# An attention stream in a hand-written order: projection matmuls moved out of the closing steps, the norm in seven pieces, subtractions moved from VectorE to GpSimd

## The chip, the cores and the metric

The kernel runs on one core of a Trainium2 chip. The metric is the device time of one execution in microseconds (us). The engines are TensorE (PE; its weight loads are listed apart as PEld), VectorE (DVE), ScalarE (ACT), GpSimd (POOL) and SyncE (SP), which here issues most DMAs. Each engine runs its own instructions strictly in the order in which the program lists them, and semaphores make one engine wait for another.

## The reference

One layer of a hybrid encoder over 16 learned "meta" tokens and 4096 tokens of width 1024. Cut to what matters:

```python
u = rmsnorm(h, norm_g)                       # h = meta tokens + x
f_in, f_gate, q, k, v, a_gate = split(u @ w_in)
f_out = fourier_branch(f_in) * silu(f_gate)  # real part of a 2-D DFT per group of 64 channels, then a mix
a_out = attention(q, k, v) * silu(a_gate)    # 8 query heads, 2 key/value heads of 64, bidirectional
h = h + concat(f_out, a_out) @ w_out
return rmsnorm(h, final_g)[:, 16:]
```

Queries and keys are normalised per head and rotated before the scores; the softmax runs over all 4112 positions. Inputs and result are float32, and the kernel reaches that precision with pairs of 16-bit numbers: a value is kept as a high part and the rest.

## The kernel before

**Phase A** (0 to about 715 us of the span) does the first norm and the input projection and writes queries, keys, values and gates to DRAM. The change does not touch it.

**The stream.** Phase B handles 8 blocks of 512 queries, and in each block four pairs of query heads: 32 pairs, `pairs = [(b, p)]`, numbered i. A pair is 66 steps j, 33 for each of its two heads, and n = j % 33. Step n = 0 takes the 16 meta keys; the other 32 steps take one tile of 128 keys each, in eight quads of four. In a quad the steps with n % 4 = 1 and 2 ("first" and "second") each open a score bank, a 128x512 float32 piece of PSUM from the pool `pq`, tag "s", which has two, with two 512-column matmuls: one with the high part of the queries (L1120) and one with their rest (L1121). Third and fourth steps (n % 4 = 3 and 0) add the difference to the key tile two steps before onto the same two banks (L1117). The fourth step is the closing one, and its numbers j are listed in `RUNS`. It also makes, in this order, two half-height matmuls for the rest of the differences (L1125), four half-height matmuls that estimate score maxima for a later pair into banks "m" of the pool `pm`, which has four (L1039), and the exponentials of both its last steps. Two relu/reduce pairs on these estimates (ACT `rl`, L1044; DVE `mx`, L1045) follow, one in the closing step, one in the next step.

Each step's exponential is an ACT instruction of 128x512 (`pe`, L1130). The part that the 16-bit `pe` loses is a subtraction `rr` of 128x512 (L1132) on DVE or POOL, as the set `on_dve` says. Five steps later (`LAG`) nine small matmuls multiply `pe` and `rr` by the values into bank `o` (L1147 to L1154). When a head ends, ACT copies `o` to `tt` (L1161), DVE makes a reciprocal and POOL four instructions on `ob`.

**Work laid between the steps.** The output projection of the previous block is 48 matmuls of 512 columns a pair (`po`, L1227) in two halves of 24, each half into one bank; DVE then takes the half out with the residual (`hh`, L1232). `OUT` lists the steps at which one projection matmul stands, right behind the step's score matmuls (`OUT0` does for pair 4, the first that has any). The final norm of the rows finished in the pair before is cut into pieces (`out_end`): a square on ACT, a guess, three Newton steps, and on DVE the scaling `yo` of 128x1024 (L1258) with the DMA out. They stand at the steps `NORM`. `out_tr` copies a pair's gated heads on ACT at step `TR` and sends them a step later through a transposing DMA (`at`, L1213) for the projection. Near the end of a pair `fin` turns the next pair's maxima into a row with one small matmul into an "m" bank (L1079), and `put` writes this row into the next queries with one copy on ACT and one on DVE (L1085, L1086).

**The Fourier branch** is a list of small entries, `flist`, filled by `f_fill` and drawn by `f_step(how many, ...)`: DFT matmuls `pd` (L858), gathers, transposes (`trans`) and mixes (`mix`: 24 matmuls, `mo` on ACT and POOL, and DMAs `mf_d` that are held until the next gather). Part of it is drawn while the first pair's maxima are made (the "startup", between phase A and the stream, `INIT` = 11 entries at a time), the rest at two or three entries a step in pairs 0 to 3 (`block0`).

The order of everything is written by hand: loop order in the code is the order on each engine. Nothing reorders it.

Of the kernel before, what the change touches and what calls it, by code (L numbers as in the profile page):

```python
# [22 lines left out]
F32 = mybir.dt.float32  # L23
# [4 lines left out]
ALU = mybir.AluOpType  # L28
# [4 lines left out]
P = 128  # L33
D = 1024
# [4 lines left out]
NT = 32  # L39
HD = 64  # L40
# [9 lines left out]
QB = 512  # L50
# [698 lines left out]
def phase_b(tc, a, pool, mm3, id32, id16, sc):  # L749
# [5 lines left out]
    V, S, T, G = nc.vector, nc.scalar, nc.tensor, nc.gpsimd  # L755
    dma, dma_t = nc.sync.dma_start, nc.sync.dma_start_transpose
# [3 lines left out]
    with ExitStack() as st:  # L760
        bp = pool(st, "bp")
        w1 = pool(st, "b1", 1)
# [3 lines left out]
        pm = pool(st, "pm", 4, PSUM)  # L766
        pq = pool(st, "pq", 2, PSUM)
# [38 lines left out]
        gts = {}  # L806
# [78 lines left out]
        def catch_up():  # L885
            while behind:
                behind.pop(0)()
# [76 lines left out]
        def f_fill():  # L964
            done = []
            for i, u in enumerate(seq):
                flist.append(("begin", i))
                flist.extend([("d", None)] * (50 if i > 8 else 52 if u is LAST else 26))
                flist.append(("gather", i))
                if i != 8:  # L970
                    done.append((len(flist), i))
                flist.extend([("gap", None)] * (12 if i == 8 else int(8 < i < 17)))

            for pos_, i in reversed(done):
                end = len(flist)
                flist.insert(min(pos_ + (21 if i < 8 else 34), end), ("t", (mix, i)))
                flist.insert(min(pos_ + (8 if i < 8 else 13), end), ("t", (trans, i)))

        f_fill()
# [115 lines left out]
        def stream(i):  # L1095
            b, p = pairs[i]
            kv = p // 2
            if p == 0:
                obs[b] = w2.tile([P, 4, 512], F32, tag="ob", name="ob")
            ob = obs[b]  # L1100
            out = []
            for e in range(2):
                h = 2 * p + e
                qa, qb = qA[b % 2][:, h], qB[b % 2][:, h]
                acc, banks = [], {}
                for t, n in enumerate(SEQ):
                    out.append(step(h, kv, t, n, qa, qb, acc, banks, ob, gts[i][:, :, e * HD:(e + 1) * HD]))
            return out

        def step(h, kv, t, n, qa, qb, acc, banks, ob, gate):  # L1110
            d = {}
            cs = slice(n * P, (n + 1) * P)

            def qk():
                if n < NT and n % 8 >= 4:
                    s = d["s"] = banks.pop(n - 4)
                    T.matmul(s, K[kv][:, 0, cs], qa, start=False, stop=False, skip_group_check=True)  # L1117
                else:
                    s = d["s"] = banks[n] = pq.tile([P, 512], F32, tag="s", name="s")
                    T.matmul(s, K[kv][:, 0, cs], qa, start=True, stop=False)  # L1120
                    T.matmul(s, K[kv][:, 1, cs], qb, start=False, stop=True)  # L1121

# [114 lines left out]
        def out_end(b, s, d):  # L1237

            xr, hh = pst.pop((b, s)), d["hh"]
            ss = sm.tile([P, 1], F32, tag="ss", name="ss")  # L1240
            rf = sm.tile([P, 1], F32, tag="rf", name="rf")

            def square():
                S.activation(xr, hh, AF.Square, accum_out=ss)

            t = sm.tile([P, 1], F32, tag="r1t", name="r1t")
            h = sm.tile([P, 1], F32, tag="r1h", name="r1h")

            def guess():
                V.tensor_scalar(out=ss, in0=ss, scalar1=1.0 / D, scalar2=EPS, op0=ALU.mult, op1=ALU.add)  # L1250
                root0(rf, ss, t, h)

            def newton():
                root1(rf, t, h)

            def scale():
                yo = w1.tile([P, D], F32, tag="yo", name="yo")
                V.scalar_tensor_tensor(out=yo, in0=hh, scalar=rf, in1=fgb[0], op0=ALU.mult, op1=ALU.mult)  # L1258
                t0 = b * QB + s * P
                dma(a["out"][t0:t0 + P], yo)  # L1260

            return square, guess, newton, newton, newton, scale

        def root0(y, x, t, h):

# [13 lines left out]

        RUNS = [33 * e + 4 * x for e in range(2) for x in range(1, 9)]  # L1280
        AHEAD = 2
        MT, TR = 60, 11
        OUT = [4] + list(range(9, 32)) + list(range(37, 61))
        OUT0 = list(range(16, 40)) + list(range(41, 65))
        NORM = [7, 11, 15, 19, 23, 28]
        fgb = []
        qload(0, (0,))
        f_step(50, 0)
# [18 lines left out]
                gload(0)  # L1307
        catch_up()
        red()
        f_step(22, 1, True)  # L1310
        catch_up()
        fin()
        f_step(12, 0, True)
        put()
        queue = []

        def draw():

            while not queue and len(ends) + 1 < len(pairs):
                i = len(ends) + 1  # L1320
                gs, meta, red, fin, put = max_units(i)
                queue.extend(gs)
                ends[i] = (meta, red, fin, put)
            return queue.pop(0) if queue else None

        ends = {}
        parts = []
        for _ in range(AHEAD):
            rest = draw()()
            catch_up()  # L1330
            for f in rest:
                f()
            f_step(INIT, 1, True)
        assert fcur["i"] >= SPARE

        def block0(g, mid):
# [25 lines left out]
        for i, (b, p) in enumerate(pairs):  # L1362
# [5 lines left out]
                load_mf(0, 0)  # L1368
            ready = {}
            halves = out_units(b - 1, p) if b > 0 else None  # L1370
            on_dve = {j for j in range(66) if j % 33 == 0 or j % 33 % 4 in (2, 3) or j % 33 % 8 == 4}
            if i + 1 == len(pairs):
                on_dve = {j for j in range(2 * NT + 2) if j % 3}
            units = stream(i)
# [2 lines left out]
                plan = dict(zip(OUT if i > 4 else OUT0, halves[0][0] + halves[0][1]))  # L1377
            for j, (qk, half, ex, pvm) in enumerate(units):
                n = j % 33
                qk()  # L1380
                if n != 4 and j in plan:
                    plan[j]()
                if j in RUNS:
                    end = pend.pop(0)() if n == 4 and pend else None
                    units[j - 1][1](0)
                    half(1)
                    more = draw()
                    if more:
                        parts.extend(more())
                    if n == 4 and j in plan:  # L1390
                        plan[j]()
                    for x in (j - 1, j):
                        units[x][2](V if x in on_dve else G)
                        if end:
                            end()
                            end = None
                    if parts:
                        parts.pop(0)()
                elif n % 4 != 3:
                    ex(V if j in on_dve else G)  # L1400
                    if parts:
                        parts.pop(0)()
# [33 lines left out]
                    low()  # L1436
                if j in NORM and prev:
                    prev[NORM.index(j)]()
                if j == (62 if i > 4 else 65) and b > 0:
                    prev = out_end(b - 1, p, halves[1])  # L1440
                pend.append(pvm)
                if len(pend) > LAG:
                    flush()
                if j == 62 and i + 1 < len(pairs):
                    fin_()
                    put_()


        b = NQB - 1
# [206 lines left out]
```

## Time and profile before

| | us |
|---|---|
| three timed runs | 3183.15 to 3186.73, median 3184.79 |
| the profiled execution | 3184.41, span 3182.6 |
| busy in the span: PE, DVE, ACT, POOL | 3094.5, 2375.6, 2028.8, 1450.6 |
| startup, 721.00 to 791.13 | 70.13 |
| pairs 0 to 3, 791.13 to 1115.74 (with the Fourier branch) | 324.61 |
| pair 4, 1115.74 to 1188.67 | 72.93 |
| pairs 5 to 30, 1188.67 to 3059.22 | 1870.55 |
| the last pair, 3059.22 to 3126.95 | 67.73 |
| tail to 3182.60 | 55.65 |

A stage runs from the first score matmul of its first pair to that of the next stage. The profile lists, for each instruction, its start and its busy time. PE matmuls are pipelined, so that a row's busy time (0.38 for 512 columns) is longer than the distance to the next matmul's start; what a matmul costs is that distance. The idle time in front of an instruction, and what ended it, stands in brackets behind its row.

### The profile page before, as it was taken

The numbers are of one execution on the slowest core, as the hardware profiler recorded it, in microseconds if no ns is written. First come the engines' busy times: TensorE is split into PE (matmuls) and PEld (weight loads), VectorE is DVE, ScalarE is ACT, GpSimd is POOL, SyncE is SP. The second block draws the span as 40 slices with busy tenths as digits, with TensorE's granted clock in tenths as the row PEclk, the third lists the DMA queues.
The fourth block names the chain that finished last, engine by engine and source line by source line (L and its number), as shares of the span: only waits on it lengthen the run. The fifth ranks groups of instructions, "written<-read, shape, count | busy, mean of one in ns | idle before, by whom it ended". The sixth has DMA issues, their size and how long they took to land.

```text
span 3182.6 us, 80710 instructions
## 1 busy us (share of the span) xinstructions
PE 3094.5 (97%) x32291; PEld 1814.6 (57%) x32291; DVE 2375.6 (75%) x5079; ACT 2028.8 (64%) x3990; POOL 1450.6 (46%) x1387
## 2 busy tenths in 40 slices
PE   7999999997999999999999999999999999999998
PEld 4555555555666655555555555555555555555554
DVE  6666566644677878888888888888888888888874
ACT  5443333325666777777777777777777777777763
POOL 4755565536344444434444444444444444444442
PEclk9999999999999999999999999999999999999999
DMA  7454444638432221111111211211121111111112
GB/s 231 156 165 142 140 176 134 197 140 226 125 86 87 82 51 32 32 28 48 38 28 28 53 33 28 51 32 28 38 48 28 28 44 42 32 31 28 28 50 69
DMA packets 237484, 243.71 MB, mean 77 GB/s; under 512 B 134306, under 2 KB 182306, under 8 KB 234162
## 3 DMA queue, kind: packets, MB, share of 16 engines
q1 hardware_dynamic: 223282, 213.37, 23.3%
q10 hardware_dynamic: 13824, 25.17, 2.1%
q8 instruction: 252, 4.13, 0.5%
q14 instruction: 126, 1.03, 0.1%
HBM read 139.59 MB, written 66.38 MB: 65 GB/s over the span
## 4 chain that ended last, share of the span: by engine, by line
PE 66%; ACT 5%; DVE 4%; DMA 2%; issue 2%; POOL 1%; SPq 0%; ACTq 0%; DVEq 0%; POOLq 0%
PE o L1147 11%; PE po L1227 8%; PE o L1154 7%; PE s L1120 7%; PE s L1117 7%; PE s L1121 6%; PE m L1039 6%; PE s L1125 5%; ACT pe L1130 3%; PE o L1152 2%; PE o L1150 2%; ACT rl L1044 2%; PE pd L858 1%; DVE yo L1258 1%; PE m L1469 1%
## 5 line engine op out<-in xcount | busy, mean ns | idle before, releaser
L1130 ACT ACTIVATE pe<-s 128x512 f32<-128x512 f32 x2112 | 1241.2, 613 | 644.1 <-PE s L1125 605.3
L1132 POOL TENSOR_TENSOR rr<-pe 128x512 f16<-128x512 f32 x766 | 811.4, 1068 | 1193.9 <-ACT pe L1130 1193.4
L1132 DVE TENSOR_TENSOR rr<-pe 128x512 f16<-128x512 f32 x1346 | 1007.7, 763 | 330.7 <-ACT pe L1130 312.4
L1154 PE MATMUL o<-VV,rr 128*128 128x65 f16 x8448 | 975.2, 193 | 0.1
L1154 PEld LDWEIGHTS <-rr 128*128 128x128 f16 x8448 | 784.8, 98 | 180.9 <-DVE rr L1132 0.2
L1147 PE MATMUL o<-VV,pe 128*128 128x129 f16 x6336 | 839.5, 221 | 0.0
L1045 DVE CUSTOM_DVE_ANT_0 rl<-m,rl 128x512 f32<-128x512 f32 x1024 | 702.1, 687 | 159.2 <-ACT rl L1044 146.7
L1147 PEld LDWEIGHTS <-pe 128*128 128x128 bf16 x6336 | 590.9, 97 | 354.7 <-issue 191.0
L1044 ACT ACTIVATE rl<-m 128x512 f32<-128x512 f32 x1024 | 630.6, 617 | 8.0 <-PE m L1039 7.2
L1120 PE MATMUL s<-qA,K 128*128 128x512 f16 x1088 | 410.7, 378 | 6.9 <-ACT pe L1130 6.5
L1121 PE MATMUL s<-qB,K 128*128 128x512 f16 x1088 | 411.3, 378 | 0.0
L1150 PE MATMUL o<-VV,pe 128*128 128x65 f16 x2112 | 411.3, 195 | 0.0
L1152 PE MATMUL o<-VV,pe 128*128 128x64 f16 x2112 | 410.6, 194 | 0.0
L1117 PE MATMUL s<-qA,K 128*128 128x512 f16 x1024 | 387.6, 378 | 10.9 <-ACT pe L1130 8.4
L309 PE MATMUL ps<-wh,xh 128*128 128x512 f16 (+2 forms) x1032 | 352.7, 354 | 8.1 <-ACT xh L297 8.0
L310 PE MATMUL ps<-wl,xh 128*128 128x512 f16 (+2 forms) x1032 | 352.6, 353 | 2.4 <-DVE wl L280 2.4
L1039 PE MATMUL m<-K,qB 64*128 64x512 f16 x1024 | 310.4, 377 | 15.3 <-DVE mx L1045 10.9
L1039 PE MATMUL m<-K,qA 64*128 64x512 f16 x1024 | 304.9, 377 | 8.0 <-ACT rl L1044 4.1
L312 PE MATMUL ps<-wh,xl 128*128 128x512 f16 x768 | 291.4, 379 | 0.0
L1152 PEld LDWEIGHTS <-pe 128*128 128x128 bf16 x2112 | 209.1, 99 | 0.0
L1150 PEld LDWEIGHTS <-pe 128*128 128x128 bf16 x2112 | 206.6, 98 | 0.0
L1125 PE MATMUL s<-qB,K 64*128 64x512 f16 x512 | 198.0, 387 | 0.0
(220 smaller groups left out, 4514.3 us busy)
## 6 DMA issues: line engine op xcount, KB each, us to landing
room<-x SPq DMA_DIRECT2D x32, 512.0 KB
xt<-xt SPq DMA_DIRECT2D x32, 512.0 KB
sg<-fx SPq DMA_DIRECT2D x16, 1024.0 KB
xr<-x SPq DMA_DIRECT2D x32, 512.0 KB
out<-yo SPq DMA_DIRECT2D x32, 512.0 KB
ct<-cdo SPq DMA_DIRECT2D x9, 1088.0 KB
fg_d<-g ACTq DMA_DIRECT2D x32, 256.0 KB
ag_d<-g ACTq DMA_DIRECT2D x32, 256.0 KB
```

Source lines behind the costliest of these rows:

```text
L1039: T.matmul(ts[x], q[e][:, 2 * p + e, s * P:(s + 1) * P], K[kv][64 * e:64 * e + 64, 0, c0:c0 + 512], start=True, stop=True)
L1044: S.activation(rl, ts[e], AF.Relu)
L1045: V.tensor_tensor_reduce(out=rl, in0=ts[2 + e], in1=rl, scale=1.0, scalar=-3.0e38, op0=ALU.add, op1=ALU.max, accum_out=mx[:, s, e, o:o + 1])
L1117: T.matmul(s, K[kv][:, 0, cs], qa, start=False, stop=False, skip_group_check=True)
L1120: T.matmul(s, K[kv][:, 0, cs], qa, start=True, stop=False)
L1121: T.matmul(s, K[kv][:, 1, cs], qb, start=False, stop=True)
L1130: S.activation(pe, d["s"], AF.Exp, scale=HD ** -0.5)
L1132: eng.tensor_tensor(out=rr, in0=pe, in1=hi, op=ALU.subtract)
L1147: T.matmul(o[:, c0:c0 + 129], hi[:, cs], va, start=t == 0 and s == 0, stop=t == NT, skip_group_check=True)
L1150: T.matmul(o[:, c0:c0 + 65], hi[:, cs], vh, start=False, stop=t == NT, skip_group_check=True)
L1152: T.matmul(o[:, c0:c0 + 64], hi[:, cs], vl, start=False, stop=t == NT, skip_group_check=True)
L1154: T.matmul(o[:, c0:c0 + 65], rr[:, cs], vh, start=False, stop=t == NT, skip_group_check=True)
```

## The change

1. `OUT` lists every step but meta and closing ones: three projection matmuls in each of a pair's sixteen quads, none in closing steps. Before, they stood at step 4, 9 to 31 and 37 to 60, closing steps included, so that a quad had four or none. There are 48 of them as before.
2. `on_dve` loses the steps with n % 8 = 4: eight subtractions a pair move from DVE to POOL (DVE 34, POOL 32 of 66). The last pair keeps its own rule.
3. The norm has seven pieces at steps 3, 7, ... 27 instead of six at 7 to 28; `scale` comes as two halves of 512 columns, and the DMA out goes behind the second.
4. `fin` and `put` go from the end of step 62 to step 63, behind its score matmuls.
5. `out_tr` goes from step 11 to 7, and with it ACT's copy, DVE's subtraction and the transposing DMA from 12 to 8.
6. In the last pair, whose heads need no maxima for a later pair, every second pair of score banks is taken from `pm`: four banks instead of two.
7. At the start a `mix` comes nine DFT entries later, unit 8 is followed by a longer gap, 22 entries drawn ahead of the first `fin` fall away, and the two first estimates for the pair after are made ahead of that `fin` instead of behind it. Fifteen DFT matmuls and one mix go by this from the startup into the stream.

```diff
-                flist.extend([("gap", None)] * (12 if i == 8 else int(8 < i < 17)))
+                flist.extend([("gap", None)] * (18 if i == 8 else int(8 < i < 17)))
...
-                flist.insert(min(pos_ + (21 if i < 8 else 34), end), ("t", (mix, i)))
+                flist.insert(min(pos_ + (30 if i < 8 else 34), end), ("t", (mix, i)))
...
-                    s = d["s"] = banks[n] = pq.tile([P, 512], F32, tag="s", name="s")
+                    late = kv and last and n < NT and n // 2 % 2
+                    s = d["s"] = banks[n] = (pm if late else pq).tile([P, 512], F32, tag="m" if late else "s", name="s")
...
-            def scale():
-                yo = w1.tile([P, D], F32, tag="yo", name="yo")
-                V.scalar_tensor_tensor(out=yo, in0=hh, scalar=rf, in1=fgb[0], op0=ALU.mult, op1=ALU.mult)
-                t0 = b * QB + s * P
-                dma(a["out"][t0:t0 + P], yo)
+            def scale(k):
+                if k == 0:
+                    d["yo"] = w1.tile([P, D], F32, tag="yo", name="yo")
+                cs = slice(k * 512, (k + 1) * 512)
+                V.scalar_tensor_tensor(out=d["yo"][:, cs], in0=hh[:, cs], scalar=rf, in1=fgb[0][:, cs],
+                                       op0=ALU.mult, op1=ALU.mult)
+                if k:
+                    t0 = b * QB + s * P
+                    dma(a["out"][t0:t0 + P], d["yo"])
...
-        MT, TR = 60, 11
-        OUT = [4] + list(range(9, 32)) + list(range(37, 61))
+        MT, TR = 60, 7
+        OUT = [j for j in range(66) if j % 33 % 4]
-        NORM = [7, 11, 15, 19, 23, 28]
+        NORM = [3, 7, 11, 15, 19, 23, 27]
...
-        f_step(22, 1, True)
-        catch_up()
-        fin()
-        f_step(12, 0, True)
-        put()
...
         for _ in range(AHEAD):
             rest = draw()()
             catch_up()
             for f in rest:
                 f()
             f_step(INIT, 1, True)
+        catch_up()
+        fin()
+        f_step(12, 0, True)
+        put()
...
-            on_dve = {j for j in range(66) if j % 33 == 0 or j % 33 % 4 in (2, 3) or j % 33 % 8 == 4}
+            on_dve = {j for j in range(66) if j % 33 == 0 or j % 33 % 4 in (2, 3)}
...
+                if n == 5 and j in plan:
+                    plan.pop(j)()
                 qk()
-                if n != 4 and j in plan:
+                if j == 63 and i + 1 < len(pairs):
+                    fin_()
+                    put_()
+                if j in plan:
                     plan[j]()
...
-                if j == (62 if i > 4 else 65) and b > 0:
+                if j == 65 and b > 0:
                     prev = out_end(b - 1, p, halves[1])
...
-                if j == 62 and i + 1 < len(pairs):
-                    fin_()
-                    put_()
```

On DVE in pair 11, around the end of its norm, the program before lists the following (each row: line, operation, output and inputs, shape; the ISA rows with `mx` are the relu/reduce, each followed by a read of its sum).

```order
L1132 TENSOR_TENSOR rr<-pe 128x512 x3
L1045 ISA rl_21706,mx<-m,rl_21706 128x512
L1045 ISA mx 128x1
L1258 SCALAR_TENSOR_TENSOR yo<-hh,rf,fgb 128x1024
L1045 ISA rl_21729,mx<-m,rl_21729 128x512
L1045 ISA mx 128x1
L1132 TENSOR_TENSOR rr<-pe 128x512
```

The changed program lists at the same place on DVE:

```order
L1134 TENSOR_TENSOR rr<-pe 128x512
L1262 SCALAR_TENSOR_TENSOR yo<-hh,rf,fgb 128x512
L1134 TENSOR_TENSOR rr<-pe 128x512
L1045 ISA rl_21632,mx<-m,rl_21632 128x512
L1045 ISA mx 128x1
L1045 ISA rl_21652,mx<-m,rl_21652 128x512
L1045 ISA mx 128x1
L1134 TENSOR_TENSOR rr<-pe 128x512
L1262 SCALAR_TENSOR_TENSOR yo<-hh,rf,fgb 128x512
```

The whole `yo` stood between the two reductions of one closing step; its halves stand in third steps, between subtractions, and both reductions come first.

On PE a closing step in the middle of pair 12 (step 16) read before, from its score matmul on:

```order
L1117 LDWEIGHTS K_6175
L1117 MATMUL s<-qA_7257,K_6175 128x512
L1227 LDWEIGHTS mt
L1227 MATMUL po<-woh,mt 128x512
L1125 LDWEIGHTS K_6175
L1125 MATMUL s<-qA_7257,K_6175 128x512
```

The changed program has there:

```order
L1118 LDWEIGHTS K_6175
L1118 MATMUL s<-qA_7257,K_6175 128x512
L1127 LDWEIGHTS K_6175
L1127 MATMUL s<-qA_7257,K_6175 128x512
L1127 LDWEIGHTS K_6175
L1127 MATMUL s<-qB_7259,K_6175 128x512
```

The projection matmul between score and rest matmuls is gone; it stands in an earlier quad that had none.

On SP, in the startup, the DMAs that take the first mix unit out (`mf_d`), the gates of the next (`fgu`) and the second block of queries (`qA`, transposed out of DRAM, and its rest `qB`) stood before in this order:

```order
L107 DMA ct_7430<-ce 128x4608
L883 DMA mf_d_64<-mo_7273 125x512
L883 DMA mf_d_64<-mo_7273 128x512
L933 DMA fgu_7434<-fg_d_62 128x512 x2
L791 DMA_TRANSPOSE qA0_7256<-q_d_59 128x4x512
L794 DMA qB0_7258<-qA0_7256 64x2x512 x2
L883 DMA mf_d_64<-mo_7273 124x512
```

And in the changed program:

```order
L107 DMA ct_7400<-ce 128x4608
L933 DMA fgu_7402<-fg_d_62 128x512 x2
L791 DMA_TRANSPOSE qA0_7256<-q_d_59 128x4x512
L794 DMA qB0_7258<-qA0_7256 64x2x512 x2
L883 DMA mf_d_64<-mo_7273 125x512
L883 DMA mf_d_64<-mo_7273 128x512
```

The first unit's `mf_d` now stands behind `fgu`, `qA` and `qB`.

More of the change, by code (lines that the diff above doesn't have):

```diff
@@ L1106, in stream, with step @@
                 for t, n in enumerate(SEQ):
-                    out.append(step(h, kv, t, n, qa, qb, acc, banks, ob, gts[i][:, :, e * HD:(e + 1) * HD]))
+                    out.append(step(h, kv, t, n, qa, qb, acc, banks, ob, gts[i][:, :, e * HD:(e + 1) * HD],
+                                    i + 1 == len(pairs)))
             return out
-        def step(h, kv, t, n, qa, qb, acc, banks, ob, gate):
+        def step(h, kv, t, n, qa, qb, acc, banks, ob, gate, last):
             d = {}
@@ L1254, in newton @@
                 root1(rf, t, h)
-            def scale():
-                yo = w1.tile([P, D], F32, tag="yo", name="yo")
-                V.scalar_tensor_tensor(out=yo, in0=hh, scalar=rf, in1=fgb[0], op0=ALU.mult, op1=ALU.mult)
-                t0 = b * QB + s * P
-                dma(a["out"][t0:t0 + P], yo)
-            return square, guess, newton, newton, newton, scale
+            def scale(k):
[7 more added lines that the diff above has]
+                    dma(a["out"][t0:t0 + P], d["yo"])
+            return square, guess, newton, newton, newton, lambda: scale(0), lambda: scale(1)
         def root0(y, x, t, h):
@@ L1309, in phase_b @@
         red()
-        f_step(22, 1, True)
-        catch_up()
-        fin()
-        f_step(12, 0, True)
-        put()
-        queue = []
+        queue, ends, parts = [], {}, []
         def draw():
@@ L1320, in draw @@
                 i = len(ends) + 1
-                gs, meta, red, fin, put = max_units(i)
+                gs, *ends[i] = max_units(i)
                 queue.extend(gs)
-                ends[i] = (meta, red, fin, put)
             return queue.pop(0) if queue else None
-        ends = {}
-        parts = []
         for _ in range(AHEAD):
@@ L1389, in phase_b @@
                         parts.extend(more())
-                    if n == 4 and j in plan:
-                        plan[j]()
                     for x in (j - 1, j):
```

## The prediction

> **What bounds the kernel now.** I read the page first, for the engines' busy times.
>
> ```profile
> span 3182.6 us, 80710 instructions
> PE 3094.5 (97%) x32291; PEld 1814.6 (57%) x32291; DVE 2375.6 (75%) x5079; ACT 2028.8 (64%) x3990; POOL 1450.6 (46%) x1387
> ```
>
> PE is busy for 97%, so one could think nothing is left. But a PE row's time is that of a pipelined matmul, and rows overlap; what PE needs must be read from start to start. So I next took the busy times by stage (after the engine's busy time, the count of instructions; after POOL the granted TensorE clock, the DMA share and GB/s).
>
> ```profile
> core 0: us, PE busy (x) PEld busy (x) DVE busy (x) ACT busy (x) POOL busy (x), PEclk, DMA share, GB/s
> 721.00:791.13 70.13, 57.96 (x538) 39.21 (x539) 35.13 (x87) 43.12 (x91) 42.79 (x26) 0.94 0.78 223
> 791.13:1115.74 324.61, 310.75 (x3882) 207.56 (x3879) 237.39 (x478) 224.43 (x450) 150.39 (x143) 0.99 0.32 97
> 1188.67:3059.22 1870.55, 1851.25 (x22004) 1068.97 (x22001) 1530.11 (x3292) 1374.06 (x2729) 778.37 (x832) 1.00 0.14 36
> 3059.22:3126.95 67.73, 63.88 (x762) 39.09 (x762) 44.62 (x63) 41.11 (x74) 31.54 (x30) 1.00 0.20 52
> 818.30:821.70 3.40, 3.40 (x27) 2.32 (x29) 0.00 (x0) 0.00 (x0) 0.00 (x0) 0.50 0.16 47
> ```
>
> The 26 steady pairs, 5 to 30, take 1870.55/26 = 71.94 each at the full clock. In them DVE is busy for 82% and ACT for 73%: an engine so full can hold PE up for short stretches. The last row is one stretch in pair 0 at half the clock; it follows a wait (below). Then the PE timeline of steps 28 to 33 of pair 11, from one closing step to the meta step of the second head (start, duration, engine, line; in brackets the idle time in front).
>
> ```profile
> 1649.96 0.38 PE L1117 MATMUL s<-qA,K 128*128 128x512 f16 x1
> ...
> 1651.62 0.38 PE L1120 MATMUL s<-qA,K 128*128 128x512 f16 x1
> ...
> 1652.05 0.38 PE L1227 MATMUL po<-woh,at 128*128 128x512 f16 x1
> 1652.27 0.22 PE L1147 MATMUL o<-VV,pe 128*128 128x129 f16 x1
> ...
> 1652.62 0.38 PE L1120 MATMUL s<-qA,K 128*128 128x512 f16 x1
> ...
> 1653.63 0.38 PE L1117 MATMUL s<-qA,K 128*128 128x512 f16 x1
> ...
> 1654.42 0.38 PE L1117 MATMUL s<-qA,K 128*128 128x512 f16 x1
> ...
> 1655.90 0.37 PE L1039 MATMUL m<-K,qB 64*128 64x512 f16 x1 [0.35 <-DVE mx L1045]
> ...
> 1656.57 0.38 PE L1120 MATMUL s<-qA,K 128*128 128x512 f16 x1
> ```
>
> This gives PE's own prices: a projection matmul 0.215 (1652.05 to 1652.27), the nine value matmuls 0.355, a first or second step with a projection 1.00, a third 0.785, a closing step 1.66 with one and so 1.44 without. A quad with three projections needs 1.00 + 1.00 + 0.785 + 1.44 = 4.225, a meta step 1.00 − 0.215 = 0.785, a pair 2 × (0.785 + 8 × 4.225) = 69.17. Both kernels issue the same matmuls, so this holds before and after; the pair takes 71.94, and 2.77 of it is waiting. The closing step at 1654.42 takes 2.15 for its 1.44.
>
> **The change part by part.** *The norm in halves.* The cause of those 0.71 stands on DVE, and the list of waits has it (sum, times, longest; idle time in front of a matmul comes out shorter than the loss, since the row before overlaps it):
>
> ```profile
> 1653.42 1.81 DVE L1258 SCALAR_TENSOR_TENSOR yo<-hh,rf,fgb 128x1024 f32<-128x1024 f32 x1
> 1655.16 0.68 DVE L1045 CUSTOM_DVE_ANT_0 rl<-m,rl 128x512 f32<-128x512 f32 x1
> PE m L1039 <- DVE mx L1045: 10.9, 29, 1.2
> ```
>
> The scaling of 1.81 stands in front of a reduction whose bank the last estimate matmul needs. In halves of about 0.9 (half of 1.81; between 0.65 and 0.95), each in a third step behind both reductions, it leaves them only their own 0.68 to do: −0.71 a pair.
>
> *The spread of projections.* Where a quad has none, its own work is 4.225 − 3 × 0.215 = 3.58, and it is the exponentials that set the pace. The rows of pair 12 from step 4 to step 8, PE and ACT:
>
> ```profile
> 1695.79 0.38 PE L1117 MATMUL s<-qA,K 128*128 128x512 f16 x1
> 1700.47 0.38 PE L1117 MATMUL s<-qA,K 128*128 128x512 f16 x1 [0.25 <-ACT pe L1130]
> 1696.94 0.60 ACT L1130 ACTIVATE pe<-s 128x512 f32<-128x512 f32 x1 [1.28 <-PE s L1125]
> 1700.24 1.11 ACT L1244 ACTIVATE xr<-hh 128x1024 f32<-128x1024 f32 x1
> ```
>
> PE takes 4.68 from the start of step 4 to that of step 8. The work of these steps here is 1.66 + 0.785 + 0.785 + 0.57 = 3.80; afterwards it is 1.44 + 1.00 + 1.00 + 0.785 = 4.225. ACT has no idle time between 1696.94 and the square at 1700.24 (exponentials, two relus, the head's copy), so I let the whole 4.68 stand: 0.46 of wait stays in each half, 0.92 a pair. The bounds are 0 and 0.92. The square, 1.11, goes from step 7 to 3, into the idle 1.28 at 1696.94, so it costs nothing; without that gap it would add up to 1.11 a pair. The other bare quads, at the ends of both halves, lose their waits by the projections that fill them.
>
> *fin and put a step later.* Step 62 of pair 12:
>
> ```profile
> 1760.40 0.38 PE L1120 MATMUL s<-qA,K 128*128 128x512 f16 x1
> ...
> 1761.43 0.38 PE L1120 MATMUL s<-qA,K 128*128 128x512 f16 x1
> ```
>
> It takes 1.03 for 0.785: `fin`'s matmul waits for an estimate bank. A step later the bank is free, and 0.06 for the matmul remains; −0.25. The query copies on ACT and DVE keep three steps before the next pair's first score.
>
> *Eight subtractions to POOL.* The same instruction on both engines (count: least, median, most, in ns):
>
> ```profile
> L1132 DVE TENSOR_TENSOR rr<-pe x1346: 670/691/3273, 792.9 to 3128.9; 128x512 f16<-128x512 f32 x193
> L1132 POOL TENSOR_TENSOR rr<-pe x766: 1029/1040/1540, 793.7 to 3127.0; 128x512 f16<-128x512 f32 x192
> 1700.55 1.04 POOL L1132 TENSOR_TENSOR rr<-pe 128x512 f16<-128x512 f32 x1
> ```
>
> DVE loses 8 × 0.69 = 5.5 a pair, POOL gains 8 × 1.04 = 8.3 on 778.37/26 = 29.9, 54% of a pair. That of step 4 would be ready at 1701.59; its value matmuls stand in step 9, after step 8's 1.44, two score matmuls and a projection: 1700.47 + 1.44 + 0.43 + 0.215 = 1702.55. The slack is 0.95, so I take 0. Bounds: −0.2 a pair (DVE's work in front of a reduction shrinks) and what the third rival says.
>
> The Trainium skill, GPSIMD Engine Reference, section 4.1 Engine selection, speaks against this part: a two-input elementwise operation belongs on VectorE, since GpSimd is about twice as slow; section 8 Key points adds that the two engines contend for SBUF where VectorE has two SBUF inputs, as here. The rows give 1.04/0.69 = 1.5, not 2; at 2 an estimate is 1.38 a piece, the slack 0.6, and the sum unchanged unless that slack is used up.
>
> *The attention copies at steps 7 and 8.* ACT's copy (group: sum, mean ns) takes the place of the longer square, so the stretch above does not grow. The transposing DMA stood behind step 12:
>
> ```profile
> L1208 ACT ACTIVATE ah<-ob 128x512 f16<-128x512 f32 x28 | 19.9, 712 | 0.0
> 1637.04 1.25 SPq L1213 DMA_TRANSPOSE at<-ah  x1
> ```
>
> It goes four steps earlier, past two steps of SP's other DMAs, and its first use goes from step 20 to 17: one step, about 1 us, more time. `mt` is used from step 1 instead of 4, nine steps and more after its DMA at step 57. Nothing for both; the bounds are 0 and the one step.
>
> Sum for a steady pair: 69.17 + 0.92 + 0.06 + 0.25 (meta estimates in one pair of four, about 1.0, as before) + 0.05 = 70.45; 1.49 × 26 = −39.
>
> *The last pair's four banks.* Its closing steps before:
>
> ```profile
> 3105.73 0.38 PE L1117 MATMUL s<-qA,K 128*128 128x512 f16 x1
> ...
> 3107.39 0.38 PE L1120 MATMUL s<-qA,K 128*128 128x512 f16 x1 [0.28 <-ACT pe L1130]
> ```
>
> 1.66 with a projection, though there are no estimates here: a third step without projection, 0.785 − 0.215, and two rest matmuls of 0.215 make 1.0. The next quad waits for the exponential that reads its bank. With four banks it need not. Own work 2 × (0.785 + 8 × (2.785 + 1.0)) = 62.1, less the last step, at whose start the stage ends, 61.1; measured 67.73. I take −6; the bounds are −6.6 and 0, if ACT sets the pace (its 41.11 of 67.73 speak against that). The tail stays.
>
> *Pairs 0 to 4.* The wait of 4.8 is one DMA for DFT tables in pair 0; the half clock behind it goes with it: 3.40 at 0.50 lose 1.7 at most, and I take 1.1, since other work lies there too.
>
> ```profile
> PE pd L858 <- DMA acs<-acs_d: 4.8, 1, 4.8
> ```
>
> Unit 9, which uses that table, now begins twelve steps later by the order of `flist` (34 instead of 22), so −6. Four `fin` at 0.3 and a few bare quads give −2.5 more. Pair 4 keeps `OUT0`: −0.3.
>
> *The startup.* The rows around its worst wait (POOL's work on a mix unit, SP's queue, ACT, PE):
>
> ```profile
> 735.81 2.36 POOL L953 TENSOR_TENSOR mo<-mo,fgu 128x1024 f32<-128x1024 f32 x1
> 741.23 3.82 SPq L791 DMA_TRANSPOSE qA<-q_d  x1
> 748.65 1.27 SPq L794 DMA_DIRECT2D qB<-qA  x2
> 750.03 7.40 DMA mf_d<-mo
> 757.53 1.20 ACT L946 ACTIVATE mo<-t 128x512 f32<-128x512 f32 x2 [5.53 <-DMA mf_d<-mo]
> 759.28 0.37 PE L1039 MATMUL m<-K,qA 64*128 64x512 f16 x1 [4.10 <-ACT rl L1044]
> ```
>
> A mix writes `mo`, which is free when an older `mf_d` has landed. Afterwards the first `mf_d` is queued on SP behind `qA` and `qB` (which waits until `qA` has landed): issue at about 749.3 (a little ahead of the 750.03 of the `mf_d` shown), landing 7.40 later, 756.7, while ACT wants that buffer at about 746. Behind ACT's `mo` stand the relus that empty PE's estimate banks, so PE waits some 8 there instead of 4.1. On the other side 15 DFT matmuls of 264 columns (0.11 each, by 0.215 for 512) and 24 small mix matmuls (0.056) leave the startup: 3.0, which the stream takes over. I put the startup with these at 0; bounds −6 and +12.
>
> All together: −39 − 6 − 8.5 − 0.3 + 0 = −54 on the profiled 3184.41, 0.4 under the median of the runs; with 1 to 2 for small collisions that a denser stream brings, −52.5, 3132.
>
> **The rivals.** *A: the startup pays.* ACT's wait for the first `mf_d` is not absorbed and the same shift recurs at the next units: +12, 3144. For it speaks the queue above; against it, that the next `mf_d` follows at once and 3.0 of work is gone. *B: waits come back.* The reductions, subtractions and halves of `yo` meet elsewhere, since DVE is still over 70% busy, and ACT, 73%, holds quads that now have three projections each: half the steady gain, +19, 3151. For it: all quads are now alike at 4.225, where ACT's stretch took 4.68; against it: at 1650 to 1654 above, quads with four projections run without a wait. *C: POOL becomes late, slower.* Every moved subtraction that comes after its value matmul holds PE; if POOL's queue is later by 0.95, each further delay falls on PE. With the whole difference 1.04 − 0.69 = 0.35 on all 8 × 27: +76, 3208. It decides from about 1 us of extra lateness a head; against it, POOL has 20 us of idle a pair. The skill's section 4.1 rule is this rival: at its 2 the price would be 8 × 27 × 0.69 = 149, an estimate; the rows bear out a ratio of 1.5. *D: better.* ACT's stretch halves (−12): 3120. That the spread does nothing is B's extreme.
>
> **How the numbers follow.** The forecast 0.64, A 0.12, B 0.13, C 0.04, D 0.07. The range 3118 to 3152 takes in D, A and B and leaves out C and larger collisions. A measurement here can tell 0.2%, 6.4 us, from no change: faster 0.95, same 0.02, slower 0.03 (C decides slower only from 58 us of loss).
>
> **What would show it.** Two `yo` of 0.65 to 0.95, the closing step before the meta step at 1.44; "m <- mx" far below 10.9; pair starts 70.2 to 70.5 apart; a last pair of about 61; no 4.8 for `acs` and no half clock near 818; ACT's wait for `mf_d` at 8 to 10 in the startup. The prediction is wrong if value matmuls wait for `rr` of POOL, or if steps 4 to 8 take more than 4.7.

## The result, and the profile after

The changed kernel takes 3138.2 us (median of four runs, 3136.3 to 3138.4) where the kernel before takes 3185.2 on the same chip: a ratio of 0.985, 95% interval 0.983 to 0.987. The forecast was 3132, so the gain was 47 where 52.5 was expected. The profiled execution took 3136.25, its span 3134.4.

The stages of the kernel after, in the same columns as before (startup, pairs 0 to 3, pair 4, pairs 5 to 30, last pair, tail):

```profile
core 0: us, PE busy (x) PEld busy (x) DVE busy (x) ACT busy (x) POOL busy (x), PEclk, DMA share, GB/s
721.00:788.70 67.70, 55.45 (x499) 37.06 (x500) 32.42 (x88) 41.57 (x89) 37.22 (x24) 0.87 0.73 199
788.70:1107.32 318.62, 311.82 (x3918) 209.75 (x3916) 226.94 (x445) 224.47 (x450) 186.28 (x176) 1.00 0.35 106
1107.32:1180.20 72.88, 71.16 (x844) 40.98 (x841) 50.87 (x108) 52.31 (x105) 39.07 (x40) 1.00 0.23 45
1180.20:3016.16 1835.96, 1834.72 (x22004) 1079.56 (x22000) 1424.82 (x3109) 1379.27 (x2729) 1029.45 (x1040) 1.00 0.14 36
3016.16:3078.78 62.62, 61.83 (x763) 38.90 (x762) 45.52 (x65) 39.80 (x74) 31.15 (x31) 1.00 0.23 56
```

| stage | before | after | difference | forecast |
|---|---|---|---|---|
| startup | 70.13 | 67.70 | −2.4 | 0 |
| pairs 0 to 3 | 324.61 | 318.62 | −6.0 | −8.5 |
| pair 4 | 72.93 | 72.88 | 0 | −0.3 |
| pairs 5 to 30 | 1870.55 | 1835.96 | −34.6 | −39 |
| last pair | 67.73 | 62.62 | −5.1 | −6 |
| tail | 55.65 | 55.62 | 0 | 0 |

The startup's −2.4 is not firm. Ten kernels below have the same startup code as the kernel after, and their profiles show 68.28 to 70.60 for it; the kernel after, at 67.70, is the shortest of them all.

A steady pair takes 1835.96/26 = 70.61, 1.33 less than before, where 1.49 was expected. The wait of the closing step 32 is gone. On PE and DVE of pair 12 in the kernel after, at the place that answers to the timeline shown of before:

```profile
1708.30 0.38 PE L1118 MATMUL s<-qA,K 128*128 128x512 f16 x1
...
1709.05 0.38 PE L1039 MATMUL m<-K,qB 64*128 64x512 f16 x1
...
1709.74 0.38 PE L1122 MATMUL s<-qA,K 128*128 128x512 f16 x1
1704.45 0.75 DVE L1262 SCALAR_TENSOR_TENSOR yo<-hh,rf,fgb 128x512 f32<-128x512 f32 x1
...
1707.45 0.69 DVE L1045 CUSTOM_DVE_ANT_0 rl<-m,rl 128x512 f32<-128x512 f32 x1 [0.28 <-ACT rl L1044]
```

Step 32 runs from 1708.30 to 1709.74, 1.44. The last half of the norm's scaling (0.75) is over at 1705.2, and the reduction at 1707.45 now waits for ACT, not for DVE's own queue.

One closing step did not come out: step 57 still takes 1.66 in the mean over the steady pairs, though its projection matmul is gone. Rows of PE, DVE and POOL of the kernel after, same pair:

```profile
1734.89 0.38 PE L1118 MATMUL s<-qA,K 128*128 128x512 f16 x1
...
1735.65 0.38 PE L1039 MATMUL m<-K,qA 64*128 64x512 f16 x1
1735.88 0.37 PE L1039 MATMUL m<-K,qB 64*128 64x512 f16 x1
...
1736.55 0.38 PE L1122 MATMUL s<-qA,K 128*128 128x512 f16 x1
1733.68 1.54 DVE L1190 TENSOR_TENSOR hl<-mf,hl 128x512 f16<-128x512 f32 x1
1735.14 0.68 DVE L1045 CUSTOM_DVE_ANT_0 rl<-m,rl 128x512 f32<-128x512 f32 x1
1732.62 2.05 POOL L1134 TENSOR_TENSOR rr<-pe 128x512 f16<-128x512 f32 x2 [2.17 <-ACT pe L1132]
```

The third and fourth estimate matmuls (half the array each) start together in step 32, at 1709.05; here the fourth starts 0.23 after the third. Its bank comes free with the reduction at 1735.14, which stands behind `hl`, DVE's share in preparing the Fourier half of the projection's input (`low` in `mf_parts`; listed in step 53, it is reached by DVE shortly before PE's step 57). It is the old fault of `yo` in another place: a long DVE instruction between two reductions. The list of waits does not show it: PE's steady pairs have no row "m <- mx" any more, since the modelled end of the third matmul covers the gap. That the projection matmul in the closing step covered this 0.22 before is tested below.

### The profile page after: what moved, and what is told of

Same layout as the page of the kernel before. It is cut to its first block, busy times and chain, and to the rows that moved or that the text cites. A ratio compares the mean times of both kernels' runs of the same rounds, so it can differ in the third digit from the quotient of the medians.

```text
span 3134.4 us, 80770 instructions
## 1 busy us (share of the span) xinstructions
PE 3074.1 (98%) x32291; PEld 1824.7 (58%) x32291; DVE 2254.5 (72%) x4861; ACT 2031.5 (65%) x3988; POOL 1741.2 (56%) x1634
## 4 chain that ended last, share of the span: by engine, by line
PE 72%; ACT 2%; DMA 1%; DVE 1%; issue 1%; POOL 0%; SPq 0%; ACTq 0%; POOLq 0%; DVEq 0%
PE o L1149 12%; PE po L1229 9%; PE o L1156 8%; PE s L1122 8%; PE s L1123 7%; PE s L1118 7%; PE m L1039 7%; PE s L1127 5%; PE o L1154 2%; PE pd L858 2%; PE o L1152 2%; PE m L1471 1%; ACT pe L1132 1%; ACT rl L1044 1%; DMA mf_d<-mo 0%
## 5 line engine op out<-in xcount | busy, mean ns | idle before, releaser
L1134 POOL TENSOR_TENSOR rr<-pe 128x512 f16<-128x512 f32 x1014 | 1126.8, 1127 | 828.2 <-ACT pe L1132 827.1
L1134 DVE TENSOR_TENSOR rr<-pe 128x512 f16<-128x512 f32 x1098 | 882.0, 807 | 289.7 <-ACT pe L1132 286.6
```

What stands on the lines that cost most here:

```text
L1134: eng.tensor_tensor(out=rr, in0=pe, in1=hi, op=ALU.subtract)
```

## The experiments

All compute the whole reference. Times are medians; the kernel after is 3138.2, and the kernel before read 3185.4 to 3187.3 beside them. Step times are starts of score matmuls, averaged over pairs 5 to 30.

### Which property of the norm's scaling cost 0.71: its size or its place?

The changed kernel with one whole scaling at step 28, between the reductions:

```diff
-        NORM = [3, 7, 11, 15, 19, 23, 27]
+        NORM = [3, 7, 11, 15, 19, 28]     # scale() in one piece, as before
```

> The changed kernel with the norm's scaling again as one instruction of 1024 columns at step 28, between the two reductions. Theory 1 (size and place of the scaling made the wait): the closing step 32 takes 2.16 again instead of 1.44, +0.72 x 27 = +19, about 3157. Theory 2 (the subtraction of step 28, now on POOL, frees 0.69 on DVE, enough for the scaling): step 32 stays at 1.44 to 1.50, time +0 to +2.

Measured 3158.5, ratio to before 0.991 (0.990 to 0.993); step 32 takes 2.20, all other steps are unchanged. DVE and POOL of pair 12 in this kernel:

```profile
1712.26 2.08 DVE L1260 SCALAR_TENSOR_TENSOR yo<-hh,rf,fgb 128x1024 f32<-128x1024 f32 x1
1714.26 0.68 DVE L1045 CUSTOM_DVE_ANT_0 rl<-m,rl 128x512 f32<-128x512 f32 x1
1711.20 2.06 POOL L1134 TENSOR_TENSOR rr<-pe 128x512 f16<-128x512 f32 x2 [2.17 <-ACT pe L1132]
```

Theory 1 holds: +20 for +0.75 x 27. The subtraction that left DVE freed nothing here. In the kernel before, `yo` took 1.81 at this place (1653.42 to 1655.23), and POOL's row next to it was

```profile
1653.12 1.04 POOL L1132 TENSOR_TENSOR rr<-pe 128x512 f16<-128x512 f32 x1 [3.38 <-ACT pe L1130]
```

In both kernels `yo` ends 1.07 to 1.08 after POOL's subtraction does. The subtraction that was moved stands on POOL in front of the other one, so that POOL, and with it `yo`, is done later.

The same whole scaling, one step earlier, behind both reductions (`NORM = [3, 7, 11, 15, 19, 27]`):

> The changed kernel with the norm's scaling as one instruction of 1024 columns, 1.8 us, but in the third step 27, behind both reductions (whole28 had it between them). Theory A (its place between two reductions made the wait): step 32 at 1.44, pair 70.6 to 70.7, time +0 to +3. Theory B (its size does): some step from 28 to 32 takes 0.3 to 0.7 more, time +8 to +19.

Measured 3139.8, ratio 0.985 (0.984 to 0.987); step 32 at 1.44, pairs at 70.64. It was the place; cutting it in halves adds nothing that shows. Its row in this kernel, and POOL's next to it:

```profile
1706.95 1.28 DVE L1260 SCALAR_TENSOR_TENSOR yo<-hh,rf,fgb 128x1024 f32<-128x1024 f32 x1
1704.31 2.06 POOL L1134 TENSOR_TENSOR rr<-pe 128x512 f16<-128x512 f32 x2 [2.17 <-ACT pe L1132]
1708.53 2.20 POOL L1134 TENSOR_TENSOR rr<-pe 128x512 f16<-128x512 f32 x2 [2.17 <-ACT pe L1132]
```

Between POOL's subtractions it takes 1.28, beside them 2.08. That POOL was out of the way is not what made the difference: in the kernel with 48 subtractions on POOL (below) the halves at steps 23 and 27 take 1.5 each instead of 0.75, and step 32 stays at 1.44.

### What are the eight subtractions worth?

The changed kernel with the old rule, subtractions of n % 8 = 4 on DVE:

```diff
-  on_dve = {j for j in range(66) if j % 33 == 0 or j % 33 % 4 in (2, 3)}
+  on_dve = {j for j in range(66) if j % 33 == 0 or j % 33 % 4 in (2, 3) or j % 33 % 8 == 4}
```

> The changed kernel with the eight subtractions a pair (steps n % 8 = 4) back on DVE. Theory of the prediction (their place costs nothing on either engine): time within 2 of the changed kernel, steady pairs 70.6. Rival 1 (DVE's load is what delayed PE, and the move carries part of the gain): steady pairs 0.2 to 0.7 longer, time +5 to +19, with waits of estimate matmuls for the reductions. Rival 2 (late subtractions on POOL cost something today): pairs shorter than 70.6.

Measured 3155.8, ratio 0.990 (0.989 to 0.992): +17.6. This is rival 1, and the prediction's zero is wrong. A steady pair takes 71.22 instead of 70.61, 15.8 in 26 pairs, and nearly all of that lies in one step: step 12 takes 2.10 instead of 1.44. In the profiles pairs 0 to 3 take 3.9 more as well, 3.0 of it in pair 3; the cause there stays open. PE and DVE there, pair 12:

```profile
1695.93 0.38 PE L1118 MATMUL s<-qA,K 128*128 128x512 f16 x1
...
1697.36 0.37 PE L1039 MATMUL m<-K,qB 64*128 64x512 f16 x1 [0.30 <-DVE mx L1045]
...
1698.03 0.38 PE L1122 MATMUL s<-qA,K 128*128 128x512 f16 x1
1695.78 0.91 DVE L1213 TENSOR_TENSOR ah<-ob,ah 128x512 f16<-128x512 f32 x1
1696.62 0.68 DVE L1045 CUSTOM_DVE_ANT_0 rl<-m,rl 128x512 f32<-128x512 f32 x1
```

The attention copy's subtraction `ah`, which the change moved to step 8, stands between two reductions too. With the subtractions on POOL, DVE is ahead by just enough for it: in the kernel after, the reduction behind `ah` ends 0.15 before step 12's fourth estimate matmul starts.

The same part alone, put into the kernel before:

> The kernel before with one part of the change alone: the eight subtractions (n % 8 = 4) on POOL. Theory (the move is worth something only where a reduction stands behind other DVE work and no projection matmul covers it; in the kernel before, the attention copies' subtraction stands at step 12 and the closing steps have projections): pairs 71.9 as before, or down to 71.7 by a shorter step 32, time 0 to -5. Rival (DVE's load costs the same in both kernels, and the move is worth the 17.6 that it cost to undo): pairs 71.3, time -17.

Measured 3186.1 beside 3187.3, ratio 0.9997 (0.9987 to 1.0006): no difference. Its step 32 goes from 2.16 to 2.20, since `yo` takes 2.08 there too, and a steady pair from 71.94 to 72.02; pairs 0 to 3 are 2.1 shorter, in one profile of each. So alone the move gains nothing; it pays where the other parts of the change make DVE late.

And further in the same direction, with every second step's subtraction on POOL as well:

```diff
+  on_dve = {j for j in range(66) if j % 33 == 0 or j % 33 % 4 == 3}
```

> The changed kernel with the subtractions of all second steps (n % 4 = 2) on POOL as well: 48 of 66 there instead of 32, in pairs 0 to 30. Theory (a subtraction on POOL is hidden as long as it lands before its value matmuls five steps later; 48 x 1.1 = 53 and the head's 5 of 70.6 still fit, and only around step 5, where the four instructions of the head's end stand, is the queue late by some tenths): pairs 70.6 to 71.0, time +0 to +10. Rival (POOL becomes the bound: two instructions of a quad late by more than the slack of about 0.9): pairs over 72, time over +40, with waits of value matmuls for rr of POOL.

Measured 3137.3, ratio 0.984 (0.983 to 0.986), pairs at 70.66: nothing. The engines of this kernel:

```profile
PE 3073.4 (98%) x32291; PEld 1825.6 (58%) x32291; DVE 1956.3 (62%) x4365; ACT 2035.1 (65%) x3988; POOL 2246.6 (72%) x2130
L1134 POOL TENSOR_TENSOR rr<-pe 128x512 f16<-128x512 f32 x1510 | 1636.2, 1107 | 398.3 <-ACT pe L1132 396.0
```

POOL has 48 subtractions a pair at 1.11 each, and PE does not notice.

### What is the spread of the projection worth?

The changed kernel with `OUT = [4] + 9..31 + 37..60` and the matmul of step 4 where it was:

> The changed kernel with the projection matmuls back at their old steps (4, 9 to 31, 37 to 60, closing steps included); all other parts of the change stay. Theory (the spread removes only the waits of bare quads on ACT): a steady pair goes from 70.61 to about 70.97, since the bare steps 5 to 8 and 61 to 64 wait again as before (0.36 a pair), and step 57 does not change (1.66, now with a projection in it); time about +9, 3147. Rival (the spread carries most of the steady gain): a pair at 71.3 or more, time +18 or more, 3156.

Measured 3153.6, ratio 0.990 (0.988 to 0.991): +15.4, pairs at 71.19. That is 0.57 a pair, between the two expectations. The theory had counted `fin`'s 0.25 as won whatever stands beside it; in the bare last quad (one without projection matmuls) it is not: steps 61 to 65 take 5.48 in this kernel and in the kernel before, with `fin` at step 63 and at 62. By place, steps 1 to 8, 34 to 41 and 61 to 65 hold 1.79 of wait a pair here and 0.99 in the kernel after, so that the spread removes 0.80; 0.22 of it comes back in step 57, which takes 1.67 here with a projection matmul in it and 1.66 in the kernel after without one.

### Step 57

The subtraction `hl` moved behind both reductions:

```diff
-  ready = dict(zip((52, 53, 55), mf_parts(*divmod(i - 3, 4))))
+  ready = dict(zip((52, 55, 56), mf_parts(*divmod(i - 3, 4))))
```

> The changed kernel with two of the three parts that prepare the Fourier half of the next projection moved: DVE's subtraction (128x512, about 1.45) from the closing step 53 to the third step 55, and its transposing DMA from 55 to 56. Theory (step 57 takes 1.66 instead of 1.44 because this subtraction stands between two reductions and the second comes too late for the fourth estimate matmul; the projection that stood in step 57 before had covered it): step 57 goes to 1.44, -0.22 a pair, time -5.7, about 3132.5. Rival (step 57 is slow for another reason, or the wait just moves on to a later step): pairs stay at 70.6 and the time within 1.

(Step 55 is a second step of its quad, not a third; it stands behind both reductions all the same.) Measured 3132.4, ratio 0.983 (0.982 to 0.985): −5.9. Step 57 takes 1.44, every other step is the same, pairs at 70.39. The group of `hl` in the kernel after and in this one (count, then busy time and mean ns):

```profile
L1190 DVE TENSOR_TENSOR hl<-mf,hl 128x512 f16<-128x512 f32 x32 | 45.6, 1426 | 0.0
...
L1190 DVE TENSOR_TENSOR hl<-mf,hl 128x512 f16<-128x512 f32 x32 | 22.5, 702 | 0.0
```

Away from POOL's pairs of subtractions it also takes half the time.

### The attention copies

The kernel of 3155.8 (subtractions on DVE) with `TR = 11` again:

> The kernel with the eight subtractions on DVE (3155.8, step 12 at 2.10) and besides the attention copies back at steps 11 and 12 instead of 7 and 8. Theory A (DVE's copy subtraction in step 8, behind the guess of the norm at 7 and ACT's stretch of steps 4 to 7, is what came too late for step 12): step 12 at 1.44, step 16 at 1.44 to 1.50, pairs 70.6, time about 3138 to 3141. Theory B (with the subtractions on DVE any instruction of 0.9 between two reductions is late, once the closing step has no projection matmul to cover it): step 12 at 1.44 but step 16 at 1.7 to 2.1, time 3146 to 3156.

Measured 3197.3, ratio 1.004 (1.002 to 1.005), slower than before, which neither theory expected. Step 12 is at 1.44, step 16 at 1.63, but step 17 takes 2.8:

```profile
PE po L1229 <- DMA at<-ah: 42.1, 27, 3.0
```

The first projection matmul that needs `at` is in step 17 since the spread; issued behind step 12 the transposing DMA comes too late in every pair. So `TR = 7` is what the spread needs, and going without it costs 41 here, net of what step 12 gains. Step 16 takes 0.19 more than its own work, its fourth estimate matmul again a little behind the third, which speaks for theory B, that an instruction of 0.9 between two reductions is late at the old DVE load wherever it stands; that is under B's bound, and with the new wait right behind it the two theories are not settled.

### The startup, the last pair and fin

The startup's order undone:

> The changed kernel with the startup's order undone (mix nine entries earlier, gap of 12 after unit 8, 22 entries and the first fin ahead of the two first estimates). Theory (the later unit 9 removed the wait of 4.8 for the DFT tables and the half clock behind it): that wait and a stretch at half clock are back in pair 0, startup and pairs 0 to 3 together take 5 to 7 more than the 67.6 + 318.6 of the changed kernel, pairs from 5 on are the same; time +5 to +7, about 3144. Rival (the gain of pairs 0 to 3 came from fin and the bare quads): no more than +2.

Measured 3143.8, ratio 0.987 (0.986 to 0.988): +5.6. Its runs lie between 3141.3 and 3145.6; the profiled one is the slowest of them and that of the kernel after its fastest, with startup and pairs 0 to 3 at 395.5 for 386.3. The wait for the tables is back, the granted clock behind it is 0.50 (820 to 825), and pair 0 takes 83.6 where the kernel after has 74.4:

```profile
PE pd L858 <- DMA acs<-acs_d: 6.3, 1, 6.3
```

All parts of the startup's order were undone together; which of them moves the wait was not tested apart.

Two parts undone in one kernel, which lie in different stages (`late = False`, and `fin`, `put` at the end of step 62):

> The changed kernel with two parts undone that lie in different stages: two score banks in the last pair, and fin and put at the end of step 62. Theory: the last pair to its last step takes 66.5 to 67.5 instead of 62.6 (closing steps 1.3 to 1.5 instead of 1.0); in the pairs ahead steps 62 and 63 together take 0.2 to 0.25 more (fin waits for an estimate bank), 6 in all; time +10 to +11, 3148. Rival for the last pair (ACT sets its pace, banks do not matter): 62.6 stays. Rival for fin (a projection in step 62 covers the wait): steps 62 and 63 stay at 2.06.

Measured 3141.7, ratio 0.986 (0.985 to 0.988). The last pair:

```profile
3016.82:3084.74 67.92, 64.01 (x762) 39.80 (x762) 43.13 (x65) 41.20 (x74) 31.00 (x31) 1.00 0.20 52
```

67.9 instead of 62.6, so the banks carry all of that stage's gain, closing steps (but for the first of each head) at 1.38 to 1.45 instead of 1.00. Steady pairs stay at 70.62: step 62 takes 1.06 and step 63 1.01, the other way round than after. Moving `fin` is worth nothing; the projection matmul in step 62 covers its wait. So the theory holds for the banks and the rival for `fin`, and the time is +3.4 instead of +10.

### A better version

The rest of the wait is in steps 4 to 7 of each half. In the kernel after, PE still takes 4.69 for 4.225 there. (As the diff shows, the changed kernel issues the projection matmul of steps 5 and 38 ahead of these steps' score matmuls, so that it counts to steps 4 and 37.)

```profile
1678.25 0.38 PE L1118 MATMUL s<-qA,K 128*128 128x512 f16 x1
...
1682.94 0.38 PE L1118 MATMUL s<-qA,K 128*128 128x512 f16 x1
```

On top of the last edit, the copy of a finished head goes from ACT to DVE, ahead of the closing step's rest matmuls:

```diff
-                    S.activation(tt, o[:, :452], AF.Copy)
+                    V.tensor_copy(out=tt, in_=o[:, :452])
...
+                    if end:
+                        end()
                     units[j - 1][1](0)
                     half(1)
```

> The kernel with the subtraction at step 55, and besides the copy of a finished head out of its bank (tt, 128x452) on DVE instead of ACT, ahead of the closing step's matmuls. Theory (in steps 4 to 7 of each half ACT sets the pace: closing step's two exponentials with the copy between them, two relus, two more exponentials; the copy is 0.43 to 0.54 of that): PE's 0.46 of wait in each half shrinks to 0.1 to 0.2, -0.5 to -0.7 a steady pair of 70.39, time -13 to -18 against 3132.4, so 3114 to 3119. Rival 1 (DVE comes late in step 8 by the copy's 0.55): steps 4 to 7 shorten, step 8 takes as much more, time within 3 of 3132. Rival 2 (PE waits there for the first exponential alone): nothing moves.

Measured 3113.7, ratio 0.977 (0.976 to 0.978): −18.6. Steps 5 and 7 go from 0.93 and 0.96 to 0.79, pairs to 69.77. The edit changes the copy's engine and its place together; the two were not tried apart. The last pair became 1.1 longer, by this:

```profile
PE o L1156 <- POOL rr L1134: 1.8, 2, 1.0
```

There the subtraction of step 3 is on POOL, and the four instructions of the head's end now stand ahead of it. This is the prediction's rival C, at two steps of one pair: steps 8 and 41 take 1.96 and 2.20 for 1.00.

Last, the projection matmul of step 6 also ahead of step 5's score matmuls, and in the last pair the subtractions of steps 3 and 36 on DVE:

```diff
-                if n == 5 and j in plan:
-                    plan.pop(j)()
+                if n == 5:
+                    for x in (j, j + 1):
+                        if x in plan:
+                            plan.pop(x)()
...
-                on_dve = {j for j in range(2 * NT + 2) if j % 3}
+                on_dve = {j for j in range(2 * NT + 2) if j % 3 or j % 33 == 3}
```

> The kernel of 3113.7 (subtraction at 55, head's copy on DVE) with two more edits: the projection matmul of step 6 also goes ahead of step 5's score matmuls, and in the last pair the subtractions of steps 3 and 36 are on DVE, so that they no longer stand behind the head's end on POOL. Theory (step 4 still has 0.14 of wait for the first exponential, which any matmul fills; in the last pair steps 8 and 41 waited 1.0 each for POOL's subtraction): -0.28 a steady pair of 69.77, -8, and the last pair 63.7 to about 61.5, -2; time about 3104. Rival (the wait goes on to step 6, which then has less work than the second exponential needs): only the last pair's -2, 3112.

Measured 3103.5, ratio 0.974 (0.973 to 0.975), 35 under the changed kernel: 7.3 less in the steady pairs and 2.2 less in the last. Its steady pairs and last pair:

```profile
2985.23:3046.80 61.57, 61.51 (x763) 38.99 (x762) 47.95 (x69) 38.96 (x72) 29.70 (x29) 1.00 0.24 57
1178.46:2985.23 1806.77, 1806.13 (x22003) 1076.32 (x22001) 1440.93 (x3161) 1353.97 (x2677) 1040.50 (x1040) 1.00 0.15 37
```

A steady pair is at 69.49, where PE's own work is 69.17. Of the rest, 0.16 are the extra meta estimates: the six pairs that hold them take 0.71 more than the others.

## Why the prediction was right or wrong

**PE's own work as the floor** held: projections, value matmuls and steps took after the change what the rows of before gave (1.00, 0.785, 1.44), and the gain is the waits that went.

**The norm, −0.71 a pair:** right in size, and undoing it costs 0.75. The text gave both the halves and the place as the means; the place alone does it.

**The stretch of steps 4 to 7, 0.92 a pair left standing:** right; 0.46 is what is left in each half. That ACT is its cause is borne out by taking the head's copy off ACT, which removed 0.31 of the 0.46 in each half.

**The eight subtractions, 0:** the step that failed. Only the slack on POOL was asked for, which is ample, and not which DVE instruction would be late without the move. The part about the attention copies counted their DMA and ACT's copy, but not DVE's subtraction, which went to step 8 between two reductions. Without the move that costs 0.66 a pair at step 12, and 17.6 in the whole time. That the two mistakes cancelled in the sum was luck.

**fin, −0.25:** the wait went, by the projection matmul in step 62; the move itself is worth 0. The text put the wait down to an estimate bank, but the bare last quad takes 5.48 wherever `fin` stands.

**The sum for a steady pair, 70.45 against 70.61:** the term that was missed is `hl` in step 57, +0.22, 5.7 in all, shown by moving it. "Where a stall goes, what is late next" was asked for `yo` alone; the other long DVE instructions between two reductions, `hl` and `ah`, lost their cover too when closing steps became 0.215 shorter. This is a small piece of rival B. With it the sum would be 70.67; the meta estimates, 0.25 in the sum, measure 0.16 after the change.

**The last pair, −6:** −5.1; what is left stands behind the start of each head: step 5 takes 1.38 and step 38 takes 1.32, with 0.785 of own work. The closing steps came to 1.00 as forecast, but not as the text adds it up, with two rest matmuls of 0.215 each. The rows of step 32 of pair 12 show what such a step holds:

```profile
1708.61 0.39 PE L1127 MATMUL s<-qA,K 64*128 64x512 f16 x1
1708.61 0.39 PE L1127 MATMUL s<-qB,K 64*128 64x512 f16 x1
1708.84 0.38 PE L1039 MATMUL m<-K,qA 64*128 64x512 f16 x1
...
1709.36 0.23 PE L1149 MATMUL o<-VV,pe 128*128 128x129 f16 x1
```

The two half-height rest matmuls start together and cost 0.22 as a pair. The other 0.2 are two changes of height: 0.31 instead of 0.215 from the score matmul at 1708.30 to the first half-height one, and 0.31 from the last half-height pair at 1709.05 to the first value matmul.

**Startup and pairs 0 to 4, −8.8 in all:** −8.5. Rival A's wait came much as worked out: the first `mf_d` is issued at 746.98 (749.3 in the text), and ACT is idle for 8.06 before its `mo`. The PE row that waits for that `mo` is a transpose (L896), not an estimate. SP, ACT and PE in the kernel after:

```profile
746.98 0.88 SPq L883 DMA_DIRECT2D mf_d<-mo  x2
...
753.24 1.24 ACT L946 ACTIVATE mo<-t 128x512 f32<-128x512 f32 x2 [8.06 <-DMA mf_d<-mo]
753.89 1.11 PE L896 MATMUL s<-id,stk 128*128 128x128 f32 x4 [6.87 <-ACT mo L946]
```

PE waits 6.87 there, and a stretch at half clock, such as left pair 0, stands behind this wait: the granted clock is 0.50 from 753.90 to 757.30, and 0.87 over the whole startup, where it was 0.94. Still the startup is not longer: the 4.1 at the relus is gone and less work stands in front of the first score. Pairs 0 to 3 took over some of it and gained 6.0, not 8.5: pair 0 became 7.0 shorter and pairs 1 to 3 together 1.0 longer (244.23 for 243.25), while with the startup's order undone they take 240.92.

**Rival C, POOL late:** not at 32, nor at 48 of 66 subtractions: no value matmul waits for POOL in the steady pairs of either kernel. POOL's idle time was more than the 20 a pair of the text; with 32 subtractions it is busy for 39.6 of 70.6. By the Trainium skill, GPSIMD Engine Reference, section 4.1 Engine selection, these two-input operations belong on VectorE, GpSimd being about twice as slow. The ratio in the rows (1.11 on POOL with 48 subtractions; 0.69 on DVE alone) is nearer 1.6 than its 2, but what decides here is that POOL had idle time and its results five steps to arrive. The Trainium skill, section 8 Key points of the same page, names contention with VectorE instructions that have two SBUF inputs. The rows agree: `hl` takes 1.43 beside POOL's subtractions and 0.70 away from them.

## What to carry to other kernels

When an engine's queue mixes short instructions that free a bank for PE with long ones, look at where the long ones stand: behind the last of a group of bank-freeing ones they cost nothing, between two of them their whole excess can land on PE. Taking filler work out of a PE step shortens the time that the other engines have there, so list every instruction that this filler was covering, not only the one that waits today. To price a part, undo it in the finished kernel and also do it alone in the old one: eight subtractions were worth 17.6 and 0.

## What the runs showed of the hardware

DVE instructions with two large SBUF inputs took up to twice as long while POOL ran its own two-input subtractions: `yo` of 128x1024 took 1.28 between them and 2.08 beside them, `hl` 0.70 and 1.43. The reductions, which read one PSUM bank and one SBUF tile, kept their 0.69. In these rows a DVE instruction that starts while a POOL subtraction runs ends a fixed time after that subtraction does, about 1.08 for `yo` (whether it took 1.81 or 2.08) and 0.55 for `hl` (1.28 in the kernel before, 1.54 after), which is most of the time that it takes alone: it looks as if it waits for POOL's instruction rather than runs beside it at a lower rate. So such an operation given to POOL is not free for DVE even when POOL's time is hidden; where it stands decides.

Two half-height matmuls of 512 columns on the two halves of the array started together and cost 0.215 us as a pair; when the second one's bank came late, in step 57, it started 0.23 behind the first. Each change between full-height and half-height matmuls cost about 0.1 us more (0.31 from start to start, where 0.215 is usual).
